# An encoder block of attention and recurrence: its woven stage put in order by estimates that also follow PSUM banks, with copies moved to ScalarE and two transfers changed

## The chip, the cores and the metric

The kernel runs on one core of one Trainium2 chip. Its metric is the device time of one execution in microseconds (us). The engines are named as in the profile: PE is TensorE (PEld its weight loads), DVE is VectorE, ACT is ScalarE, POOL is GpSimd, and SP is the queue that issues the transfers.

## What is computed

One layer on a sequence of 1024 positions with 1024 channels, in float32. A combined projection feeds two branches. Their sum, gated, is merged and added to the input, and a gated feed-forward part with a convolution of width 3 follows.

```
h = rms_norm(x, norm_mix_g)
mla_cols, rw_cols, gate_cols = split(h @ w_in)
o_a = mla_branch(mla_cols, ...)      # 8 heads: softmax(q k' + rope) v over all 1024 positions
o_b = rwkv7_branch(rw_cols, ...)     # 8 heads of 64: a forward and a backward scan,
...                                  #   state = state*w + (state a) b' + v k',  out = state r
y = sig(gA) * (o_a @ w_o[:512]) + sig(gB) * (o_b @ w_o[512:])
x = x + y @ w_merge
x = x + (silu(dwconv(h2 @ w_ffn_gate)) * (h2 @ w_ffn_up)) @ w_ffn_down     # h2 = rms_norm(x)
```

## The kernel before

The work has three stages. First come the projections and what prepares both branches. The second stage, which starts where `written` is entered (line 785) and ends at line 1628, weaves two things into one order of instructions: the **recurrence** and the **dense work**. The third is the merge and the feed-forward part; nothing in it is changed.

**Dense work** is the generator `dense`: the last gate projections (`gates`), then `attention` (line 1264), then `branch0` (line 1422), the first branch's product with the output weights `w_o`. Large products are split: a float32 operand x goes in as a rounded part `hi` and a remainder `lo`, and three matmuls hi·hi, hi·lo, lo·hi replace one. Attention takes 8 heads with 16 steps each (two halves of the queries by 8 blocks of keys). A step multiplies keys by queries into a PSUM bank `st` (three of them), ACT takes the exponential, and DVE or POOL forms the remainder `pl` of the rounded probabilities `ph`. Four steps later (`LAG`, line 48) `values` (line 1268) multiplies both by the values into the one bank `po`. On odd steps ACT takes the exponential twice, into `ph` and in place, and DVE subtracts; on even steps ACT writes the exponential `pe` into a buffer `wraw`, rounds it into `ph`, and POOL subtracts. At a head's last block the sum of values is copied out of `po` to `pv` by DVE and its logarithm to `rc` by ACT (lines 1283 and 1284).

While a head runs, `maxima` (line 1238) finds the row maxima for the next head: 16 products into banks `sc`, each reduced by DVE (`mx`), two in each of the steps 3 to 10; in step 11 a small DVE maximum and in step 12 a transpose on PE, after which ACT writes the negated maxima `mr`. They go by one transfer to a buffer `dm` in DRAM (line 1257) and by a second into row 96 of the next head's queries `qh` (line 1258). The next head's queries and keys are loaded in step 0 of a head (`load_h`, line 1219).

**The recurrence** runs over 8 units of 128 positions. For each, `prep_a` (line 834) makes decays and the inverse of a triangular matrix, the last part of it in four small steps on PE that the planner calls p, x, y and t; they write `TT`, `U` and `Y`, and their results are copied out of the banks alternately by DVE and ACT (lines 946, 957, 967). `prep_b` (line 971) makes further operands (`Er`, `Ek`, `BT`). `chain` (line 1035) is the serial part, 7 hops a unit, with results in banks of the same ring `sc` (four banks, line 800) under the name `ct`; one hop copies both halves of the new state out of `ct`, one half by DVE into `RR[0]` and the other by ACT into `RR[1]`. `gnorm` (line 1115) normalizes the unit's output `osb`: a product into `sc`, two activations there by ACT (`rsqrt_`), four multiplications and an addition by DVE, a product with the gates' weights, and from unit 4 on a sum and a split whose last part goes out of `osb` to `d_ob` in DRAM.

**The order** is fixed when the program is written: PE, DVE, ACT and POOL get their instructions in exactly the order in which these generators issue them. The planner at line 1580 picks the next piece by a model of time. `now` is PE's time; the wrapper `Clocked` (line 91) adds each DVE, ACT or POOL instruction's estimated duration to that engine's time, and `Fed` (line 111) notes when a matmul's operands are ready. A job of the preparation is due when its operands are estimated ready; a hop of the chain when its input is ready and enough dense work (`DENSE`) has gone by; otherwise the next dense piece is taken (`fill`). `dense_at` is the time at which the next `values` has its operands. If it lies later than `now[0] + 200`, dense work counts as blocked, and hops and heavy preparation steps go first. The model knows nothing of banks that are still occupied, and nothing of transfers. SP's order is not written by hand here; its instructions still wait in a line, each for its own data or buffer.

Of the kernel before, what the change touches and what calls it, by code (L numbers as in the profile page):

```python
# [10 lines left out]
F32 = mybir.dt.float32  # L11
# [55 lines left out]
DENSE_MIN = 1300  # L67
CT_BUFS = 2

# [17 lines left out]
def block_kernel(ctx: ExitStack, tc: tile.TileContext, a):  # L87
    nc = tc.nc
    now, ends, needs_pe, wrote = [0.0], [0.0], [0.0], {}

    class Clocked:


        def __init__(self, eng, fixed, each):
            self.eng, self.fixed, self.each, self.t = eng, fixed, each, 0.0

        def __getattr__(self, name):
            f = getattr(self.eng, name)

            def call(*args, **kw):  # L100
                o = kw["in_"] if name == "tensor_reduce" else kw["out"] if "out" in kw else args[0] if args else None
                if hasattr(o, "shape"):
                    out = kw["out"] if "out" in kw else args[0]
                    names = [x.tensor.name for x in (*args, *kw.values()) if x is not out and hasattr(x, "tensor")]
                    self.t = max(self.t, now[0], *(wrote.get(x, 0) for x in names)) + self.fixed + self.each * math.prod(o.shape[1:])
                    ends[0] = max(ends[0], self.t)
                    wrote[out.tensor.name] = self.t
                return f(*args, **kw)  # L108
            return call

    class Fed:
# [5 lines left out]
        def __getattr__(self, name):  # L117
            f = getattr(self.eng, name)

            def call(out, a, b, **kw):  # L120
                needs_pe[0] = max(needs_pe[0], wrote.get(a.tensor.name, 0), wrote.get(b.tensor.name, 0))
                wrote[out.tensor.name] = 0
                return f(out, a, b, **kw)  # L123
            return call

    E = Fed(nc.tensor)
    V, S, G = Clocked(nc.vector, 140, 1.04), Clocked(nc.scalar, 140, 0.92), Clocked(nc.gpsimd, 100, 2.35)
    mult, add, sub = ALU.mult, ALU.add, ALU.subtract
# [114 lines left out]
    def rsqrt_(out, ss, scale, bias):  # L243
        act(out, ss, AF.Ln, scale=scale, bias=bias)
        act(out, out, AF.Exp, scale=-0.5)
# [542 lines left out]
    now[0] = V.t = S.t = G.t = 0.0  # L788
    wrote.clear()
    wpool["g"] = ctx.enter_context(pool("gp", side="right"))  # L790
# [43 lines left out]
    def prep_a(n, q):  # L834
# [109 lines left out]
        for g in range(4):  # L944
            r, b = 32 * g, 32 * (g % 2)
            (S.copy if g % 2 else V.tensor_copy)(TT[r:r + 16, :, b + 16:b + 32], py[r:r + 16])
        yield 1600, 300
# [7 lines left out]
        for h in range(2):  # L955
            ib = slice(h * 64 + 32, h * 64 + 64)
            (S.copy if h else V.tensor_copy)(Y[ib], p3[ib])
        yield 1100, 300
# [6 lines left out]
        for h in range(2):  # L965
            ia = slice(h * 64, h * 64 + 32)
            (S.copy if h else V.tensor_copy)(TT[ia, :, 32:64], p3[ia])
        q.update(TT=TT)
# [66 lines left out]
    def chain(n, q, osb):  # L1035
# [30 lines left out]
        for i in range(2):  # L1066
# [14 lines left out]
            for s, d, c in EACH:  # L1081
                for hs in H:
                    E.matmul(ct[hs, s, :], TT[hs, 8 * i + s, :], rh[hs, s, :], start=(s == 0), stop=(s == 7))
            V.tensor_copy(RR[0][H[0], :, 1, :], ct[H[0]])
            S.copy(RR[1][H[1], :, 1, :], ct[H[1]])
# [29 lines left out]
    def gnorm(n, osb):  # L1115
        if n == NU // 2:
            xb.extend([[place(f"h{x}{4 + p}", f"ob{x}") for x in "hl"] for p in range(NPAIR - 1)])
        for d in range(2):
# [13 lines left out]
            if n >= NU // 2:  # L1132
                ob = wk.tile([128, 512], F32, tag="gsq", name="gob")
                nc.sync.dma_start(ob.rearrange("p (c t) -> p c t", t=128), d_obf[:, :, cs])
            rsqrt_(ps, ps, 1.0 / 64, gneps)
            rs = osb[:, d, :].rearrange("p (c t) -> p c t", t=128)
            for p in range(NPAIR):
                V.scalar_tensor_tensor(out=rs[:, p], in0=rs[:, p], scalar=vc("lng", p), in1=ps[:, 128 * p:128 * p + 128], op0=mult, op1=mult)
            V.tensor_tensor(out=b3, in0=rs if d == 0 else rs[:, :, ::-1], in1=b3, op=add)
            yield 540, 300  # L1140
            ps = scb()
# [96 lines left out]
    def maxima(h):  # L1238
        qh, kh = qk[h % 2]
        pt = scb  # L1240
        mx2 = eq.tile([128, 8, 2], F32, tag="mx2", name="mx2")
        for qt in range(8):
            for i2, hs in enumerate(halves()):
                ps = pt()
                E.matmul(ps, qh[0:96, qt * 128:(qt + 1) * 128], kh[0:96, hs], start=True, stop=True)
                V.tensor_reduce(out=mx2[:, qt, i2:i2 + 1], in_=ps, axis=AX_X, op=ALU.max)
                yield 213
        mx = eq.tile([128, 8], F32, tag="mx", name="mx")
        V.tensor_tensor(out=mx, in0=mx2[:, :, 0], in1=mx2[:, :, 1], op=ALU.max)
        yield 0  # L1250
        pm = pt()
        E.transpose(pm[0:8, 0:128], mx, ident)
        eq.tile([128, 8], F32, tag="pad", name="pad")
        mr = eq.tile([8, 128], R, tag="mr", name="mr")
        S.activation(mr, pm[0:8, 0:128], AF.Copy, scale=-1.0)
        dm = dr.tile([8, 128], F32, tag="dm", name="dm", bufs=2)
        nc.sync.dma_start(dm, mr.bitcast(F32))
        nc.sync.dma_start(qh[96:97, :].bitcast(F32), dm.rearrange("a b -> (a b)")[None, :])
        yield 213

    o0, o3 = [], []
    dense_at = [0.0]

    def attention():
# [3 lines left out]
        def values(h, q2, kt, ph, pl):  # L1268
# [10 lines left out]
            if kt == 7:  # L1279
                if i == 0 and q2 == 0:  # L1280
                    po["v"], po["r"] = (place(x, n, F32, [128, 2, 512]) for x, n in (("hl7", "pv"), ("hh7", "rc")))
                pv, rc = po["v"][:, q2], po["r"][:, q2]
                V.tensor_copy(pv[own], po[0][own])
                act(rc[own], po[0][oth], AF.Ln)
                po["t"] = max(V.t, S.t)
                if i == 1:
# [23 lines left out]
        def low():  # L1310
            eng, pl, x, ph = lows.pop(0)
            eng.tensor_tensor(out=pl, in0=x, in1=ph.bitcast(F32), op=sub)

        for h in range(8):
            qh, kh = qk[h % 2]
            nxt = maxima(h + 1) if h < 7 else iter(())
            for q2 in range(2):
                qs = HT[q2]
                for kt in range(8):
# [9 lines left out]
                    cost = 640  # L1329
                    for _ in range(2 if 3 <= step < 11 else 1 if step in (11, 12) else 0):  # L1330
                        cost += next(nxt, 0)
# [11 lines left out]
                    else:  # L1343
                        ph, pl = (wpool["g3"].tile([128, 512], R, tag=t, name=n) for t, n in (("gt", "ph"), ("gl", "pl")))
                    if npl[0] % 2:
                        act(ph, ps, AF.Exp)
# [16 lines left out]
                    if len(late) == LAG and late[0][2]:  # L1363
                        after()
                    yield cost
        low()
        queue.extend([lambda br=br, j=j: wrows(w_o(br, j), 0, NPAIR) for br, j in [*((0, j) for j in range(8)), (1, 0)]])
        for i in range(LAG):
# [9 lines left out]
    def wrows(src, k, n):  # L1378
        return wload(src[:, k * 128:min(k + 4, n) * 128], 128 * min(4, n - k), bufs=2)

    def w_o(br, j):
# [88 lines left out]
    LATER = ("er", "ak", "bt")  # L1470
    HEAVY = ("nm", "nz", "p", "x", "y", "t", "er", "ak", "bt")
    seen = {}
    due, hops, ready = 0.0, 0, 0.0
# [18 lines left out]
    class Job:  # L1492
# [5 lines left out]
        def due(self):  # L1498

            step, _, eng = self.steps[self.k]  # L1500
            t = max(self.at, eng.t - SLACK if eng else 0)
            if self.i:
# [77 lines left out]
    for u in range(NU):  # L1580
        osb = None if u else wk.tile([128, 2, 512], F32, tag="osb", name="osb")
        ch = chain(u, qs_[u], lambda: osb)
        for k in range(9):
            want = [(u, None, "t"), (u, 0, "bt")] if k == 0 else [(u, 1, "bt")] if k == 3 else []
            sparse = 0
            while True:
                t = max([ready] + [seen.get(x, math.inf) for x in want])
                thin = sparse_()
                blocked = dense_at[0] > now[0] + 200
                if t <= now[0] and (blocked or due <= 0 and not thin):  # L1590
# [616 lines left out]
```

## Time and profile before

| | us |
|---|---|
| median of 3 runs (lowest, highest) | 1910.35 (1905.93, 1911.68) |
| profiled execution, its own time | 1902.57 |
| its span, first to last instruction | 1900.8 |

The page gives each engine's busy time and, in 40 slices of 47.5 us, how busy it was; the line PEclk is the share of TensorE's full clock that was granted. The recurrence lies from about 366 to 1063 us of the span, attention from about 631 to 1024 us, and the product with `w_o` follows. Of the chain of work that ended last, only the part from 953 us on is a single thread; in the woven stage PE is nearly always the engine at work, and the question there is when PE stands still.

### The profile page before, as it was taken

The page shows a single profiled execution, that of the slowest core. Times are in us where ns is not written, and L with a number is a line of the kernel's source. Part 1 is how long each engine was busy: PE and PEld are TensorE (multiplying, and loading weights), DVE is VectorE, ACT ScalarE, POOL GpSimd, SP SyncE. Part 2 cuts the span into 40 slices and gives each one's busy share as a digit, 9 for nine tenths or more (in the row PEclk, how much of TensorE's full clock was granted, in tenths as well). Part 3 has the DMA queues.
Part 4 walks back from the last instruction along what each step waited for, and adds up shares of the span by engine and source line. Part 5 has one row for each costly group of instructions (what it writes and reads, how often), then busy time and mean ns, then how long its engine had stood idle before and what let it go on. Part 6 is the DMA issues. An engine that isn't in the chain of part 4 may idle for free. (4 is left out here: it accounts for less than half of the span.)

```text
span 1900.8 us, 36763 instructions
## 1 busy us (share of the span) xinstructions
PE 1821.6 (96%) x14928; PEld 1457.5 (77%) x14928; DVE 1214.8 (64%) x1867; ACT 865.6 (46%) x1387; POOL 634.1 (33%) x559
## 2 busy tenths in 40 slices
PE   8899999999999998988998999999999999999998
PEld 6666667888787877766776877878888888888886
DVE  5956666445566686767573363688675766757667
ACT  5776566223233466655666544543332323323231
POOL 2434555322222324352533322336223222222221
PEclk9999999999999899998999999999999999999999
DMA  4146444844455445453434682111111111111112
GB/s 171 45 145 221 159 161 161 239 134 106 131 142 139 125 107 146 103 141 84 98 93 146 206 300 81 63 49 56 50 51 51 54 63 51 50 51 51 59 47 105
DMA packets 260633, 210.65 MB, mean 111 GB/s; under 512 B 127145, under 2 KB 205033, under 8 KB 260465
## 3 DMA queue, kind: packets, MB, share of 16 engines
q1 hardware_dynamic: 260464, 208.31, 36.4%
q8 instruction: 117, 1.92, 0.4%
q14 instruction: 52, 0.42, 0.1%
HBM read 144.64 MB, written 59.41 MB: 107 GB/s over the span
## 5 line engine op out<-in xcount | busy, mean ns | idle before, releaser
L108 POOL TENSOR_TENSOR wlo<-wraw,whi 128x512 fp32r<-128x512 f32 x118 | 164.1, 1391 | 564.0 <-ACT whi L108 561.7
L123 PE MATMUL st<-hh,whi 128*128 128x512 f32 x408 | 170.6, 418 | 10.3 <-ACT hh L108 8.6
L123 PE MATMUL st<-hl,whi 128*128 128x512 f32 x408 | 162.5, 398 | 0.5 <-DVE hl L108 0.5
L108 DVE TENSOR_TENSOR x<-b,x 128x512 f32<-128x512 f32 x176 | 119.0, 687 | 53.4 <-PE b L123 53.4
L123 PE MATMUL st<-hh,wlo 128*128 128x512 f32 x408 | 139.5, 396 | 0.6 <-POOL wlo L108 0.6
L108 POOL TENSOR_TENSOR pl<-pe,ph 128x512 fp32r<-128x512 f32 x64 | 83.1, 1301 | 162.6 <-ACT ph L108 134.0
L108 ACT CAST whi<-wraw 128x512 fp32r<-128x512 f32 x118 | 72.9, 618 | 133.7 <-issue 39.0
L123 PEld LDWEIGHTS st<-hh,whi 128*128 128x128 f32 x408 | 77.9, 191 | 37.3 <-issue 10.4
L108 DVE TENSOR_REDUCE mx<-sc 128x1 f32<-128x512 f32 x128 | 81.9, 683 | 27.2 <-PE sc L123 27.0
L123 PEld LDWEIGHTS st<-hh,wlo 128*128 128x128 f32 x408 | 78.1, 192 | 18.5 <-POOL wlo L108 1.0
L123 PEld LDWEIGHTS st<-hl,whi 128*128 128x128 f32 x408 | 78.2, 192 | 16.9 <-issue 1.2
L108 POOL TENSOR_TENSOR wl<-wraw,wh 128x512 fp32r<-128x512 f32 x22 | 28.9, 1314 | 173.1 <-ACT wh L108 173.1
L108 DVE TENSOR_TENSOR u<-b,p 128x512 f32<-128x512 f32 x42 | 29.0, 691 | 70.6 <-PE b L123 70.6
L123 PE MATMUL b<-sl,wh 128*128 128x512 f32 x176 | 68.6, 390 | 0.8 <-DVE sl L108 0.8
L123 PE MATMUL b<-sh,whi 128*128 128x512 f32 x176 | 68.6, 390 | 0.7 <-DVE x L108 0.7
L123 PE MATMUL b<-sh,wh 128*128 128x512 f32 x176 | 68.6, 390 | 0.6 <-ACT sh L108 0.6
L123 PE MATMUL b<-sh,wl 128*128 128x512 f32 x176 | 68.5, 389 | 0.0
L123 PE MATMUL b<-sh,wlo 128*128 128x512 f32 x176 | 68.5, 389 | 0.0
L123 PE MATMUL b<-sl,whi 128*128 128x512 f32 x176 | 68.5, 389 | 0.0
L108 DVE TENSOR_TENSOR pl<-st,ph 128x512 fp32r<-128x512 f32 x64 | 43.7, 685 | 29.7 <-ACT st L108 29.4
L108 ACT CAST whi<-s 128x512 fp32r<-128x512 f32 x33 | 20.6, 623 | 87.2 <-PE b L123 87.2
L123 PE MATMUL po<-ph,vhh 128*128 128x512 f32 x128 | 57.2, 447 | 1.8 <-ACT rc L108 1.8
(488 smaller groups left out, 5298.1 us busy)
## 6 DMA issues: line engine op xcount, KB each, us to landing
wraw<-w_in SPq DMA_DIRECT2D x64, 256.0 KB
wraw<-w_fd SPq DMA_DIRECT2D x44, 256.0 KB
AA<-w_fu SPq DMA_DIRECT2D x41, 256.0 KB
A<-w_fg SPq DMA_DIRECT2D x41, 256.0 KB
d_gate<-gt SPq DMA_DIRECT2D x32, 256.0 KB
ld<-d_x SPq DMA_DIRECT2D x32, 256.0 KB
xt<-xT SPq DMA_DIRECT2D x8, 512.0 KB
d_s<-sg SPq DMA_DIRECT2D x8, 512.0 KB
```

What stands on the lines that cost most here:

```text
L108: return f(*args, **kw)
L123: return f(out, a, b, **kw)
```

## The change

1. **The model of time.** Each tile of the tags `sc`, `st`, `po`, `whi` and `wlo` belongs to a ring of so many buffers (`RING`); `slot` gives the time at which the tile that had the same buffer before was last used, and an instruction or matmul that writes a tile is now estimated to start no earlier. A job whose step needs a bank (`BANKS`) is not due before `vacant("sc")`. DVE and POOL instructions with two operands in SBUF are modelled as excluding each other (`port`).
2. **The planner's test for blocked dense work** becomes `dense_at[0] > now[0] - 800` in place of `+ 200`: operands must be estimated ready for 0.8 us.
3. **`gnorm`** gives way (`yield 540, 0`) between the two activations and DVE's multiplications, and the planner comes back to it when ACT is estimated done.
4. **Copies go to ACT alone**: those of p to t (`TT`, `Y`), the half of the state that DVE copied (`RR[0]`), and `pv`.
5. **Maxima**: `mr` is written to row 96 of `qh` by one transfer, without `dm`. The transpose is issued in the first step after 11 in which the last maximum is estimated ready, and in step 14 at the latest.
6. **Output weights**: in the last four steps of attention (the two even ones among them) the remainder is formed from PSUM by DVE, so that `wraw` is free, and the first block of `w_o` is loaded after step 5 of the last half head; its split (`wsplit`) takes the place in the queue at which it was loaded before.

The diff, cut to its core:

```diff
-CT_BUFS = 2
+RING = {"sc": 4, "st": 3, "po": 1, "whi": 2, "wlo": 2}
...
+    def slot(t):
+        if t.name not in prior:
+            tag = t.tag.split("_")[0]
+            q, n = order.setdefault(tag, []), RING.get(tag, 0)
+            prior[t.name] = q[-n] if 0 < n <= len(q) else None
+            q.append(t.name)
+        return used.get(prior[t.name], 0)
+    def vacant(tag):
+        q = order.get(tag, [])
+        return used.get(q[-RING[tag]], 0) if len(q) >= RING[tag] else 0
...
-                    self.t = max(self.t, now[0], *(wrote.get(x, 0) for x in names)) + self.fixed + self.each * math.prod(o.shape[1:])
+                    self.t = max(self.t, now[0], slot(out.tensor), *(wrote.get(x, 0) for x in names))
...
+                    if shared:
+                        self.t = max([self.t] + [e for b, e in self.port[1 - self.side] if b <= self.t])
+                        begin = self.t
+                    self.t += self.fixed + self.each * math.prod(o.shape[1:])
...
-                needs_pe[0] = max(needs_pe[0], wrote.get(a.tensor.name, 0), wrote.get(b.tensor.name, 0))
+                needs_pe[0] = max(needs_pe[0], slot(out.tensor), wrote.get(a.tensor.name, 0), wrote.get(b.tensor.name, 0))
...
-            (S.copy if g % 2 else V.tensor_copy)(TT[r:r + 16, :, b + 16:b + 32], py[r:r + 16])
+            S.copy(TT[r:r + 16, :, b + 16:b + 32], py[r:r + 16])
...
-            (S.copy if h else V.tensor_copy)(Y[ib], p3[ib])
+            S.copy(Y[ib], p3[ib])
...
-            (S.copy if h else V.tensor_copy)(TT[ia, :, 32:64], p3[ia])
+            S.copy(TT[ia, :, 32:64], p3[ia])
...
-            V.tensor_copy(RR[0][H[0], :, 1, :], ct[H[0]])
+            S.copy(RR[0][H[0], :, 1, :], ct[H[0]])
...
             rsqrt_(ps, ps, 1.0 / 64, gneps)
+            yield 540, 0
...
-            yield 540, 300
+            yield 0, 300
...
-        dm = dr.tile([8, 128], F32, tag="dm", name="dm", bufs=2)
-        nc.sync.dma_start(dm, mr.bitcast(F32))
-        nc.sync.dma_start(qh[96:97, :].bitcast(F32), dm.rearrange("a b -> (a b)")[None, :])
+        nc.sync.dma_start(qh[96:97, :].bitcast(F32), mr.bitcast(F32))
...
-                V.tensor_copy(pv[own], po[0][own])
+                S.copy(pv[own], po[0][own])
...
-                    for _ in range(2 if 3 <= step < 11 else 1 if step in (11, 12) else 0):
+                    for _ in range(2 if 3 <= step < 11 else 1 if step == 11 or step > 11 and mx_at[0] <= now[0] + cost or step == 14 else 0):
...
-                    if npl[0] % 2:
+                    if npl[0] % 2 or h == 7 and q2 and kt > 3:
...
+                    if h == 7 and q2 and kt == 5:
+                        raw = wpool["w"].tile([128, 512], F32, tag="wraw", name="wraw")
+                        wpool["load"] = nc.sync.dma_start(raw, w_o(0, 0))
...
-        queue.extend([lambda br=br, j=j: wrows(w_o(br, j), 0, NPAIR) for br, j in [*((0, j) for j in range(8)), (1, 0)]])
+        queue.append(lambda: wsplit(raw))
+        queue.extend([lambda br=br, j=j: wrows(w_o(br, j), 0, NPAIR) for br, j in [*((0, j) for j in range(1, 8)), (1, 0)]])
...
-            t = max(self.at, eng.t - SLACK if eng else 0)
+            t = max(self.at, eng.t - SLACK if eng else 0, vacant("sc") if step in BANKS else 0)
...
-                blocked = dense_at[0] > now[0] + 200
+                blocked = dense_at[0] > now[0] - 800
```

More of the change, by code (lines that the diff above doesn't have):

```diff
@@ L89, in block_kernel, with __init__ @@
     now, ends, needs_pe, wrote = [0.0], [0.0], [0.0], {}
+    used, order, prior = {}, {}, {}
+    def slot(t):
[8 more added lines that the diff above has]
+        return used.get(q[-RING[tag]], 0) if len(q) >= RING[tag] else 0
     class Clocked:
-        def __init__(self, eng, fixed, each):
-            self.eng, self.fixed, self.each, self.t = eng, fixed, each, 0.0
+        def __init__(self, eng, fixed, each, port=None, side=0):
+            self.eng, self.fixed, self.each, self.t, self.port, self.side = eng, fixed, each, 0.0, port, side
         def __getattr__(self, name):
@@ L104, in call @@
                     names = [x.tensor.name for x in (*args, *kw.values()) if x is not out and hasattr(x, "tensor")]
-                    self.t = max(self.t, now[0], *(wrote.get(x, 0) for x in names)) + self.fixed + self.each * math.prod(o.shape[1:])
+                    self.t = max(self.t, now[0], slot(out.tensor), *(wrote.get(x, 0) for x in names))
+                    data = [str(kw[x].tensor.space) for x in ("in0", "in1") if hasattr(kw.get(x), "tensor")]
+                    shared = self.port is not None and len(data) == 2 and "PSUM" not in data
+                    if shared:
+                        self.t = max([self.t] + [e for b, e in self.port[1 - self.side] if b <= self.t])
+                        begin = self.t
+                    self.t += self.fixed + self.each * math.prod(o.shape[1:])
+                    if shared:
+                        self.port[self.side].append((begin, self.t))
+                        del self.port[self.side][:-8]
                     ends[0] = max(ends[0], self.t)
                     wrote[out.tensor.name] = self.t
+                    for x in (out.tensor.name, *names):
+                        used[x] = max(used.get(x, 0), self.t)
                 return f(*args, **kw)
@@ L120, in call @@
             def call(out, a, b, **kw):
-                needs_pe[0] = max(needs_pe[0], wrote.get(a.tensor.name, 0), wrote.get(b.tensor.name, 0))
+                needs_pe[0] = max(needs_pe[0], slot(out.tensor), wrote.get(a.tensor.name, 0), wrote.get(b.tensor.name, 0))
+                for x in (a, b, out):
+                    used[x.tensor.name] = max(used.get(x.tensor.name, 0), now[0], needs_pe[0])
                 wrote[out.tensor.name] = 0
@@ L126, in block_kernel @@
     E = Fed(nc.tensor)
-    V, S, G = Clocked(nc.vector, 140, 1.04), Clocked(nc.scalar, 140, 0.92), Clocked(nc.gpsimd, 100, 2.35)
+    port = ([], [])
+    V, S, G = Clocked(nc.vector, 140, 1.04, port, 0), Clocked(nc.scalar, 140, 0.92), Clocked(nc.gpsimd, 100, 2.35, port, 1)
     mult, add, sub = ALU.mult, ALU.add, ALU.subtract
@@ L788, in block_kernel @@
     now[0] = V.t = S.t = G.t = 0.0
-    wrote.clear()
+    for x in (wrote, used, order, prior):
+        x.clear()
+    for x in port:
+        x.clear()
     wpool["g"] = ctx.enter_context(pool("gp", side="right"))
@@ L1249, in maxima @@
         V.tensor_tensor(out=mx, in0=mx2[:, :, 0], in1=mx2[:, :, 1], op=ALU.max)
+        mx_at[0] = wrote[mx.tensor.name]
         yield 0
@@ L1255, in maxima @@
         S.activation(mr, pm[0:8, 0:128], AF.Copy, scale=-1.0)
-        dm = dr.tile([8, 128], F32, tag="dm", name="dm", bufs=2)
-        nc.sync.dma_start(dm, mr.bitcast(F32))
-        nc.sync.dma_start(qh[96:97, :].bitcast(F32), dm.rearrange("a b -> (a b)")[None, :])
+        nc.sync.dma_start(qh[96:97, :].bitcast(F32), mr.bitcast(F32))
         yield 213
     o0, o3 = [], []
-    dense_at = [0.0]
+    dense_at, mx_at = [0.0], [0.0]
     def attention():
@@ L1282, in values @@
                 pv, rc = po["v"][:, q2], po["r"][:, q2]
-                V.tensor_copy(pv[own], po[0][own])
+                S.copy(pv[own], po[0][own])
                 act(rc[own], po[0][oth], AF.Ln)
-                po["t"] = max(V.t, S.t)
+                po["t"] = S.t
                 if i == 1:
@@ L1379, in wrows, with wsplit @@
         return wload(src[:, k * 128:min(k + 4, n) * 128], 128 * min(4, n - k), bufs=2)
+    def wsplit(raw):
+        hi, lo = (wpool["w"].tile([128, 512], R, tag=t, name=t, bufs=2) for t in ("whi", "wlo"))
+        split(raw, hi, lo)
+        return hi, lo
     def w_o(br, j):
@@ L1471, in block_kernel @@
     HEAVY = ("nm", "nz", "p", "x", "y", "t", "er", "ak", "bt")
+    BANKS = ("nm", "nz", "p", "x", "y", "t", "er", "ak", "bt")
     seen = {}
```

## The prediction

> **What bounds the kernel now.** I read the page's busy shares first, then a table of stretches, then PE's own list of waits, then the waits of ACT and DVE that lie behind those.
>
> ```profile
> PE 1821.6 (96%) x14928; PEld 1457.5 (77%) x14928; DVE 1214.8 (64%) x1867; ACT 865.6 (46%) x1387; POOL 634.1 (33%) x559
> ```
>
> ```profile
> 366.00:1063.10 697.10, 662.38 (x9992) 533.19 (x9987) 426.26 (x842) 343.07 (x618) 222.17 (x243) 0.97 0.48 124
> 640.00:1020.00 380.00, 353.71 (x5055) 281.11 (x5053) 265.45 (x501) 237.66 (x438) 147.50 (x155) 0.97 0.44 108
> ```
>
> The page says that PE is busy for 96% of the span, so the kernel is bound by PE's work, which the change leaves as it is. What can be won lies in the woven stage. The first row of the second block is that stage, the second its part with attention (start and end, length, then PE, PEld, DVE, ACT and POOL, the granted clock, the share and rate of the transfers). PE stands still for 697.1 - 662.4 = 34.7 us of the stage; 380 - 353.7 = 26.3 us of it lie in attention. A granted clock of 0.97 over 697 us costs 0.03 x 697 = about 21 us more (17 to 24 with the rounding). So about 56 us is the most that any order of this stage could win, 3% of the kernel.
>
> PE's own waits, from just before the stage (320 us) to 1100 us, say who ended each stop (total us, how often, longest):
>
> ```profile
> PE sc L123 <- issue: 6.9, 3, 3.1
> PE sc L123 <- DMA qh<-d_qrh: 6.2, 3, 4.0
> PE st L123 <- ACT whi L108: 4.7, 1, 4.7
> PE sc L123 <- DVE mx L108: 4.1, 3, 2.2
> PE sc L123 <- ACT osb L108: 4.0, 1, 4.0
> PE po L123 <- DVE pl L108: 1.9, 2, 1.4
> PE po L123 <- ACT rc L108: 1.8, 2, 1.6
> PE sc L123 <- ACT gsq L108: 1.2, 1, 1.2
> PE sc L123 <- DMA Un<-dU: 1.1, 1, 1.1
> ...
> PE po L123 <- POOL pl L108: 0.6, 1, 0.6
> PE sc L123 <- ACT RR L108: 0.5, 1, 0.5
> ```
>
> I sort them in three. One stop of 4.7 us is the first output weight. DVE `mx`, DVE and POOL `pl`, ACT `rc`, `gsq` and `RR`, together 4.1 + 1.9 + 0.6 + 1.8 + 1.2 + 0.5 = 10.1 us, are matmuls issued before a result was there or before a bank was empty: this is what the planner's model of time decides. The rest, 6.9 + 6.2 + 4.0 + 1.1 = 18.2 us, are instructions that waited for nothing visible and transfers, of which the model knows nothing, before or after.
>
> A stop costs more than its length:
>
> ```profile
> 856.50:866.70 10.20, 9.62 (x55) 7.45 (x57) 8.01 (x19) 5.58 (x12) 1.27 (x1) 0.50 0.11 26
> 887.20:890.60 3.40, 3.25 (x8) 2.50 (x9) 2.20 (x4) 0.00 (x0) 1.11 (x1) 0.50 1.08 221
> 1023.70:1027.10 3.40, 2.91 (x8) 1.87 (x10) 0.00 (x0) 1.96 (x4) 2.55 (x2) 0.50 1.03 417
> ```
>
> These three stretches stand right behind the three stops of 4 us and more (`osb`, `qh<-d_qrh`, `whi`). In each the clock is granted at 0.50, for 10.2, 3.4 and 3.4 us, so half of that, 5.1, 1.7 and 1.7 us, is lost on top. [...]
>
> **The change part by part.** *Output weights (part 6).* Time of start, duration, engine, instruction:
>
> ```profile
> 1018.70 0.38 SPq L220 DMA_DIRECT2D wraw<-w_o  x1
> ...
> 1023.52 0.62 ACT L108 CAST whi<-wraw 128x512 fp32r<-128x512 f32 x1 [4.84 <-DMA wraw<-w_o]
> ...
> 1024.19 2.08 PE L123 MATMUL st<-o,whi 128*128 128x512 f32 x4 [4.74 <-ACT whi L108]
> ```
>
> The load goes out at 1018.70, is rounded 4.8 us later, and PE stands for 4.74 us. Issued after step 5 of the last half head, some three steps before attention's end, the load can land before PE needs it. The stop and its clock are worth 4.7 + 1.7 = 6.4 us. Behind it the second weight block and the second operand (`o` of 1 MB) come next, on the same transfers; so I take 5, with 1 and 6.4 as ends. That DVE forms two of the remainders which POOL made costs it 2 x 0.68 us (first row below, shortest, median and longest in ns), beside other work.
>
> ```profile
> L108 DVE TENSOR_TENSOR pl<-st,ph x64: 673/682/693, 636.2 to 1016.0; 128x512 fp32r<-128x512 f32 x64
> ```
>
> ```profile
> L108 DVE COPY pv<-po x16: 673/688/695, 669.1 to 1019.5; 64x512 f32<-64x512 f32 x16
> ```
>
> ```profile
> L108 DVE COPY Y<-sc x8: 683/683/684, 413.9 to 1016.7; 32x512 f32<-32x512 f32 x8
> L108 ACT COPY Y<-sc x8: 578/579/582, 414.6 to 1017.4; 32x512 f32<-32x512 f32 x8
> ```
>
> *Copies on ACT (part 4).* The waits of ACT and DVE on each other, and the copies themselves:
>
> ```profile
> ACT TT L108 <- DVE TT L108: 53.2, 23, 9.6
> ACT RR L108 <- DVE RR L108: 42.0, 14, 6.4
> ...
> ACT rc L108 <- DVE pv L108: 20.8, 14, 4.2
> ...
> ACT Y L108 <- DVE Y L108: 13.7, 8, 5.4
> ```
>
> ```profile
> L108 DVE COPY TT<-sc x24: 411/422/680, 409.5 to 1029.4; 16x256 f32<-16x256 f32 x16, 32x512 f32<-32x512 f32 x8
> L108 ACT COPY TT<-sc x24: 363/366/583, 409.9 to 1030.1; 16x256 f32<-16x256 f32 x16, 32x512 f32<-32x512 f32 x8
> ```
>
> ```profile
> L108 DVE COPY RR<-ct 64x512 f32<-64x512 f32 x16 | 10.8, 678 | 8.0 <-PE ct L123 8.0
> ...
> L108 ACT COPY RR<-ct 64x512 f32<-64x512 f32 x16 | 9.3, 582 | 42.1 <-DVE RR L108 42.0
> ```
>
> ACT's copy waits for DVE's of the same bank nearly every time: 53.2 + 42.0 + 20.8 + 13.7 = 129.7 us in 59 waits, in which the exponentials queued behind it wait too. Put on one engine the pair needs no such wait. ACT takes on 16 x 0.37 + 8 x 0.58 (`TT`) + 8 x 0.58 (`Y`) + 16 x 0.58 (`RR`) + 16 x 0.58 (`pv`, of the same size as `RR`) = 34 us; DVE gives up 16 x 0.42 + 8 x 0.68 + 8 x 0.68 + 16 x 0.68 + 16 x 0.68 = 39 us. In attention ACT is busy 237.7 of 380 us; if two thirds of the 34 us fall there, it comes to 260, or 69%, which still leaves room. Two copies one behind the other take 1.16 us where DVE and then ACT took 0.68 + 0.58 = 1.26 and a semaphore: no loss for the chain. By itself this is worth nothing on PE beyond the waits counted above; it makes the estimates easier to keep.
>
> [...] Where two such copies ran beside each other, one engine would be slower; here the wait rows say that they ran one after the other. This is a rival below.
>
> *`gnorm` gives way (part 3).*
>
> ```profile
> DVE osb L108 <- ACT sc L108: 54.9, 15, 9.1
> ```
>
> DVE stood 15 times, 3.7 us on average, before the multiplications until ACT had done its two activations, with `mx`, `pl` and copies of banks queued behind them. After the change the planner puts other DVE work there. It is what stands behind several of the `mx` and `pl` stops.
>
> *Banks in the model, and the 0.8 us (parts 1 and 2).* They aim at the 10.1 us of my second group, by filling with recurrence work until the operand is there. The estimates will not always hold; I take two thirds, 6.5 us. From both sides: none of it, or all 10.1 us. The clock of the stage besides the three stretches quoted has lost 21 - 8.5 = 12 us in shorter stops and phases of small matmuls; I take 2 of that, and 0 and 6 as ends.
>
> *Maxima (part 5).*
>
> ```profile
> SPq L1258 <- DMA dm<-mr: 8.0, 7, 1.4
> ```
>
> SP, whose queue holds the loads of keys, queries and values, stands 8.0 us in 7 waits for the first of the two transfers to land. That goes. PE never waits for row 96 by the list above, so the transfer itself is worth nothing; SP's release may shorten the 6.2 us of `qh<-d_qrh`, but `load_h` is issued two or three steps later. I take 1 us, with 0 and 3 as ends. A transpose that is issued as late as step 14 leaves two steps until the next head reads row 96. Two steps last 6 us on average (380 us for 128 of them), more than the 4.8 us of the weights' load, so mostly nothing is late; I take a loss of 0.5, with 0 and 7 (1 us at each of seven head changes) as ends.
>
> *The third group, 18.2 us, and its clock.* New order deals these anew. The 4.0 us for `osb` came when ACT had to wait for the store of the unit before; with its 5.1 us of clock it is 9.1 us, in one place. A norm with one more step per direction ends neither clearly earlier nor later. I take 2 us as a gain here, with a loss of 6 and a gain of 9 as ends.
>
> **Sum.** 5 + 6.5 + 2 + 1 - 0.5 + 2 = 16 us. Against the profiled execution's own 1902.6 us this is 1886.6. That execution lay 7.8 us under the median of the runs, 1910.35, by which I forecast: 1894. What a measurement of this kernel can tell from no change is about 0.3%, or 5.7 us.
>
> **The rivals.**
>
> *The stops move instead of going.* The planner still sees no transfer, and the third group is larger than the second. If the two groups trade places, only the output weights and SP's waits are left: 1910.35 - 6 = 1904, or with half of them given back 1907. For it speaks that 18.2 of 34.7 us idle are outside the model; against it, that DVE's 54.9 us and ACT's 129.7 us in line go for a reason that is not a matter of luck.
>
> *Slower: bare steps at the change of heads.*
>
> ```profile
> 882.96 0.58 SPq L1223 DMA_DIRECT2D qh<-d_qrh  x1
> ...
> 887.35 1.19 PE L123 MATMUL sc<-kh,qh 96*128 96x512 f32 x2 [3.99 <-DMA qh<-d_qrh]
> ```
>
> The next head's queries are asked for in step 0 and read in step 3; here the load took 4.4 us from its issue, and PE stood 3.99 us. With the new test blocked dense work lets hops and preparation run earlier, so the recurrence gets ahead and has less left to lay between the steps 0 and 3 of later heads. Each such change then costs 4.0 + 1.7 = 5.7 us. There are six changes of heads with such a load; if all six stood bare, that is 34.2 less the 6.2 + 1.7 of now, 26 us more, and 1894 + 26 = 1920. At the fifth bare change the gain of 16 is gone (5 x 5.7 - 7.9 = 20.6); only all six give a loss over 5.7 us. Against it:
>
> ```profile
> L108 ACT COPY osb<-ct x16: 581/587/589, 436.7 to 1062.4; 128x512 f32<-128x512 f32 x16
> ```
>
> the recurrence's last output leaves its bank at 1062.4 us, 38 us behind the first product with `w_o` at 1024.19, so there is work left over to the end, and the model, now with waits for banks in it, holds jobs back as well as forward.
>
> [...] If the pairs of copies could have run side by side, one engine alone makes 16 `RR` pairs longer by 1.16 - 0.68 = 0.48 us, 16 pairs of long `TT` and `Y` copies the same (8 + 8), and 16 short pairs by 0.73 - 0.42 = 0.31 us: 15.4 + 5.0 = 20 us. If all of that came onto PE, 1894 + 20 = 1914. The 59 waits speak against it.
>
> *The change doesn't do what it says:* the early load could stay behind others in SP's queue (before, it went out at 1018.70 behind two loads and a store), and then 5 of the 16 us are missing: 1899.
>
> **How the numbers follow.** The forecast and its neighbour without the early weights hold 0.70, both over 5.7 us faster; the moved stops 0.17, of which 0.03 lie just beyond the bound on the fast side; bare head changes 0.09; ACT as the bound 0.04, of which 0.01 stays within the bound. The best case takes every gain's end, but of the clock only the 2: 6.4 + 10.1 + 9 + 3 + 2 = 30.5, or 1880. On the other side I reach to 1912, which takes in the moved stops and leaves out bare head changes and the worst of ACT. So 1880 to 1912; faster 0.73, same 0.15, slower 0.12.
>
> **What would show it.** Right: PE's list without the stop before the first `st<-o,whi` and with `mx`, `pl` and `rc` under 4 us together; no wait of ACT for DVE on `TT`, `RR`, `rc`, `Y`; DVE's wait for ACT before `osb` under 15 us; PE idle in the woven stage near 23 us with a clock of 0.98. Wrong: stops for `qh<-d_qrh` or for row 96 that grew, a long stop at `osb`, or PE's idle time unchanged with other names in the list. Were the three named groups gone and the time still the same, the clock or the small matmuls would hold what I ascribe to waiting.

## The result and the profile after

The kernel after takes 1917.51 us (median of 8 runs, 1914.12 to 1920.98), beside 1909.66 us for the kernel before (8 runs, 1903.23 to 1912.77). The ratio is 1.0054, with a 95% interval of 1.0038 to 1.0070: the change made the kernel about 8 us slower, where a gain of 16 us was forecast. The profiled execution of after took 1914.12 us with a span of 1912.3 us, 11.5 us more than the span of before.

The first part of the page of after gives each engine's busy time:

```profile
PE 1827.0 (96%) x14928; PEld 1463.4 (77%) x14928; DVE 1177.4 (62%) x1805; ACT 896.8 (47%) x1451; POOL 629.2 (33%) x557
```

PE issues the same 14,928 matmuls. DVE gave up 37 us and ACT took on 31 us, as worked out beforehand (39 and 34). So the difference has to be sought in when PE stands still and at what clock it runs. Two tables of stretches, first of before, then of after, each with the whole woven stage (first `sc` to first `b`) and with attention (first `st<-qh,kh` to first `st<-o,whi`):

```profile
365.68:1089.13 723.45, 688.73 (x10113) 554.43 (x10113) 437.62 (x862) 360.02 (x642) 231.57 (x254) 0.97 0.48 127
631.20:1024.19 392.99, 362.51 (x5240) 288.15 (x5239) 272.02 (x511) 243.31 (x449) 150.08 (x157) 0.97 0.45 111
```

```profile
369.56:1102.63 733.07, 691.65 (x10108) 558.11 (x10107) 401.31 (x802) 391.85 (x706) 227.83 (x252) 0.97 0.48 126
629.60:1035.22 405.62, 376.34 (x5658) 303.01 (x5656) 253.65 (x480) 270.06 (x503) 147.65 (x156) 0.95 0.44 108
```

The stage grew by 9.6 us. PE stands still for 733.07 - 691.65 = 41.4 us of it, before for 723.45 - 688.73 = 34.7 us. The rest is clock: half-clock stretches cover 51.2 us of the stage in after, 41.0 us in before (10 and 7 stretches), and half of each is counted as lost, 25.6 against 20.5 us (a little too much, since PE also stands still in some of them). Idle time and lost clock together grew by 6.7 + 5.1 = 11.8 us, which more than covers the stage's 9.6. The 3.9 us by which the stage starts later are not the change's: its start lies between 365.7 and 370.6 us over all 18 traces, whatever the version; what follows the stage took 2.0 us less, and so the span grew by 11.5.

PE's own waits in after, from 320 to 1110 us (total us, how often, longest):

```profile
PE sc L151 <- issue: 10.3, 6, 2.6
PE sc L151 <- DVE mx L134: 7.7, 6, 2.6
PE sc L151 <- DMA qh<-d_qrh: 4.2, 3, 1.8
PE sc L151 <- ACT osb L134: 2.9, 1, 2.9
PE st L151 <- DMA qh<-mr: 2.8, 2, 2.0
PE st L151 <- issue: 2.6, 2, 1.9
PE b L151 <- ACT obh L134: 2.6, 1, 2.6
PE st L151 <- ACT pe L134: 2.5, 1, 2.5
PE po L151 <- POOL obl L134: 2.2, 1, 2.2
PE ct L151 <- ACT RR L134: 1.1, 2, 0.7
PE po L151 <- ACT rc L134: 1.1, 1, 1.1
```

The stop before the first output weight is gone, but `mx`, which the model of banks was to shorten, went from 4.1 to 7.7 us, "issue" from 6.9 to 12.9, and there are new names: `qh<-mr`, `obh`, `pe`, `obl`. Before, 8 stops of the stage lasted over 1.5 us; now 12 do. All of PE's waits for another engine's result together, without the weights' and ACT's `osb`, went from 12.9 to 18.7 us by the full lists.

The waits of DVE and ACT on each other did go, as foreseen. From their lists in after:

```profile
DVE osb L134 <- ACT sc L134: 17.6, 4, 9.4
```

```profile
ACT TT L134 <- PE sc L151: 34.3, 11, 8.0
ACT RR L134 <- PE sc L151: 23.7, 13, 3.4
```

DVE's 54.9 us before the multiplications of `gnorm` became 17.6. ACT's copies to `TT`, `RR` and `Y` now wait for PE alone; no wait for DVE on `TT`, `RR`, `rc` or `Y` is left. So these parts of the change did what they say, and PE still stands longer.

### The profile page after: what moved, and what is told of

Its sections match the earlier page's. It is cut to its first block, busy times and chain, and to the rows that moved or that the text cites. A ratio compares the mean times of both kernels' runs of the same rounds, so it can differ in the third digit from the quotient of the medians.

```text
span 1912.3 us, 36801 instructions
## 1 busy us (share of the span) xinstructions
PE 1827.0 (96%) x14928; PEld 1463.4 (77%) x14928; DVE 1177.4 (62%) x1805; ACT 896.8 (47%) x1451; POOL 629.2 (33%) x557
## 3 DMA queue, kind: packets, MB, share of 16 engines
q8 instruction: 117, 1.92, 0.4%
## 4 chain that ended last, share of the span: by engine, by line
PE 71%; DVE 5%; DMA 2%; issue 2%; ACT 2%; POOL 1%; SPq 1%; ACTq 0%; POOLq 0%; DVEq 0%
PE b L151 37%; PE st L151 13%; PE sc L151 10%; PE po L151 7%; PE ct L151 4%; DVE x L134 1%; DMA qh<-d_qrh 1%; DVE u L134 1%; DVE wlo L134 0%; DMA y<-d_gate 0%; DVE mx L134 0%; DVE b L134 0%; DVE wl L134 0%; DMA d_obf<-gbo 0%; DMA wraw<-w_in 0%
## 5 line engine op out<-in xcount | busy, mean ns | idle before, releaser
L151 PE MATMUL st<-qh,kh 128*128 128x512 f32 x128 | 57.1, 446 | 5.5 <-DMA qh<-mr 2.8
L134 ACT CAST whi<-s 128x512 fp32r<-128x512 f32 x33 | 20.5, 623 | 87.2 <-PE b L151 87.2
```

## The experiments

Two theories stood at first: the loss comes from the new order of PE, or it comes from the edits themselves (a longer chain on ACT, a transpose too late). Then, with the order found to be at fault, two more: the model of banks makes bad orders (A1 in the texts on record), or any newly planned order is a draw from a wide scatter (A2).

All times are medians beside the kernel before on the same chip (1906.2 to 1909.1 us over four groups of runs). "Idle" is PE's idle time in the woven stage, "lost clock" half of its half-clock stretches, both of the profiled execution.

### Edits and order apart

The change edits instructions and also lets the planner choose another order. To part the two, the planner's choices were recorded as a list of pieces and the kernel follows the list instead of choosing:

```diff
-                blocked = dense_at[0] > now[0] + 200
...
-                x = prepare(not blocked and (thin or sparse and t < math.inf), not blocked and 0 < alone[0] < BATCH and due > -math.inf)
...
+            while (p := next(plan)) != "c":
+                norm.run() if p == "n" else fill() if p == "f" else jobs[ord(p) - 65].run()
```

PE's list of instructions in after differs from that of before: some 1500 instructions stand in another place. With the list of before, every one stands where it stood. **e1** is before with its own order as a list.

> The kernel before, with its sequence of pieces written out as a list in place of the planner's choices; every engine's order is unchanged. Both theories: 1909 us, within 0.3% of before. Its profile tells which stops of PE come back from run to run at the same place (those that the order makes) and which do not: I expect the stops for osb, qh and the first output weight again within 0.5 us, and stops that wait for nothing visible at other places or of other lengths.

It took 1909.39 us, ratio 0.9999 (0.9981 to 1.0017): within that interval the list itself costs nothing. **e2** holds PE's order of before and has the edits that need no new order: the copies on ACT (part 4), the maxima by one transfer (of part 5, without the later transpose), the early output weights (part 6).

```diff
-            V.tensor_copy(RR[0][H[0], :, 1, :], ct[H[0]])
+            S.copy(RR[0][H[0], :, 1, :], ct[H[0]])
...
-        nc.sync.dma_start(dm, mr.bitcast(F32))
-        nc.sync.dma_start(qh[96:97, :].bitcast(F32), dm.rearrange("a b -> (a b)")[None, :])
+        nc.sync.dma_start(qh[96:97, :].bitcast(F32), mr.bitcast(F32))
...
+                        wpool["load"] = nc.sync.dma_start(raw, w_o(0, 0))
```

> The pieces in exactly the order of before on PE, with the edits alone: copies on ACT, maxima by one transfer (transpose in step 12 as before), early output weights. Theory A (the new order is what costs, the edits by themselves win): about 1903 us, 6 less than before, the stop of 4.7 us before the first product with the output weights gone. Theory B (copies on ACT cost, by ACT's longer line): about 1917 us, with ACT's exponentials late in PE's list.

It took 1892.47 us, ratio 0.9904 (0.9873 to 0.9936), less than either theory had expected. **e3** is the reverse: PE's order of after as a list, with the copies, the two transfers and the late output weights of before.

> The pieces in exactly the order of after on PE, with the old copies, two transfers for the maxima and the late output weights. Theory A: slower than after by what the edits win, about 1923 us. Theory B: faster than after, about 1909 us.

It took 1928.16 us, ratio 1.0093 (1.0068 to 1.0118). The four corners, in us (ratios above; after with its own order is the 1.0054 of the result):

| | order of before | order of after |
|---|---|---|
| edits of before | 1909 | 1928 (e3) |
| edits of after | 1892 (e2) | 1918 |

The edits gain in either order, 16 us in the old and 11 us in the new one. The new order costs 19 us without them and 25 us with them. (After was timed beside another chip's kernel before. By the ratios, which compare on one chip, the edits gain 18 and 7 us, and the order costs 18 and 29.) PE's waits in e2 over the same 320 to 1110 us, and its attention as a stretch:

```profile
PE sc L123 <- DMA qh<-d_qrh: 5.9, 3, 4.0
PE sc L123 <- issue: 4.8, 2, 2.5
PE sc L123 <- ACT osb L108: 4.6, 1, 4.6
PE sc L123 <- DMA Un<-dU: 2.0, 1, 2.0
PE po L123 <- DVE pl L108: 1.4, 1, 1.4
PE sc L123 <- ACT gsq L108: 1.2, 1, 1.2
PE po L123 <- POOL pl L108: 1.1, 1, 1.1
...
PE st L123 <- ACT whi L108: 0.6, 1, 0.6
...
PE sc L123 <- DVE mx L108: 0.4, 1, 0.4
PE ct L123 <- ACT RR L108: 0.3, 1, 0.3
```

```profile
634.08:1013.26 379.18, 361.16 (x5241) 289.23 (x5239) 251.70 (x472) 263.69 (x489) 147.68 (x155) 0.97 0.46 113
```

All stops over 1 us that e2 still has, but for one of 1.06 us (`pl`), stood at the same places before; `mx` fell from 4.1 to 0.4 us, `rc` from 1.8 to nothing, the output weights from 4.7 to 0.6. Idle time in attention fell from 392.99 - 362.51 = 30.5 to 379.18 - 361.16 = 18.0 us. PE's order is untouched, so this is only operands, banks and weights that were there earlier.

The waits speak against the rival with ACT as the bound, in which the pairs of copies could have run side by side: with the copies dealt to both engines, as in e3, ACT's list shows

```profile
ACT TT L134 <- DVE TT L134: 54.2, 23, 8.4
...
ACT RR L134 <- DVE RR L134: 29.8, 13, 4.2
```

and in the order of before the edits that put them on one engine are part of the 16 us won (e2; the copies were not run apart from the other two edits).

**e4** is after with the old test, planned anew.

```diff
-                blocked = dense_at[0] > now[0] - 800
+                blocked = dense_at[0] > now[0] + 200
```

> After, with the planner's test for blocked dense work as before (+ 200 in place of - 800); the planner chooses anew. If the 0.8 us are what costs: about 1909 us, and the clock lost in attention back from 20 to near 10 us. If the order costs for another reason (banks in the model, or any new deal): 1915 to 1920 us, as after.

1923.45 us, ratio 1.0071 (1.0049 to 1.0094). Without the 0.8 us the planner dealt no better order; how much one such deal can tell, the later runs show.

### Is it the model of banks?

**e5** has the edits of e2, but the planner of before chooses again. The edits alone, above all the copies' new engine, change its choices.

> The edits (copies on ACT, maxima by one transfer, early weights) with the planner of before, which chooses its order anew since the copies changed engines. Theory A1 (the new model of banks makes the bad order): about 1893 us, as with the old order held fixed. Theory A2 (the old order was a lucky one, and any new deal by either planner lands some 10 to 25 us above it): 1903 to 1918 us.

1907.23 us, ratio 0.9999 (0.9977 to 1.0022). The same instructions as e2, the same planner as before, and the 16 us are gone: merely dealing the order again cost them. **e6** adds part 3, `gnorm`'s extra step.

```diff
+            yield 540, 0
...
-            yield 540, 300
+            yield 0, 300
```

> The same and the norm giving way before DVE's multiplications, still with the old model and the old test. A1: 1888 to 1893 us, since DVE's wait for ACT before osb goes. A2: anywhere from 1895 to 1918 us.

1923.15 us, ratio 1.0080 (1.0056 to 1.0103), with this row at the head of PE's waits:

```profile
PE sc L123 <- DMA qh<-d_qrh: 21.8, 4, 11.8
```

This is the rival of bare steps at the change of heads; it is real, but it struck here and not in after, where that wait is 4.2 us. **e7** is after without its model of banks: nothing is held to wait for a bank or a port.

```diff
-        return used.get(prior[t.name], 0)
+        return 0
...
-        return used.get(q[-RING[tag]], 0) if len(q) >= RING[tag] else 0
+        return 0
...
-    V, S, G = Clocked(nc.vector, 140, 1.04, port, 0), Clocked(nc.scalar, 140, 0.92), Clocked(nc.gpsimd, 100, 2.35, port, 1)
+    V, S, G = Clocked(nc.vector, 140, 1.04), Clocked(nc.scalar, 140, 0.92), Clocked(nc.gpsimd, 100, 2.35)
```

> After, without the model's part for rings, vacant banks and the shared port; the test at 0.8 us, the norm and all edits stay. A1: about 1893 us, 25 less than after. A2: no nearer to 1893 than after is, 1905 to 1920.

1890.86 us, ratio 0.9910 (0.9886 to 0.9935). **e8** keeps the model and takes the other planning parts back (+200, the old `gnorm`, the old transpose steps).

> The edits with the new model of banks alone: the test at + 200, the norm and the step of the transpose as before. A1: about 1917 us, as after. A2: 1903 to 1918 us, not clearly apart from the other deals.

1941.83 us, ratio 1.0183 (1.0154 to 1.0212). Two pairs now said that the model costs 27 us (e7 to after) and 35 us (e5 to e8). That looked like the cause; the next runs were made to test it.

### Or is any new order a draw?

In what follows a constant of the planner is changed by 30 ns: the estimated time of a hop (`HOP`) or the margin on a result (`MARGIN`), both 300 ns. The work on the chip stays the same; the planner merely chooses differently here and there. **e9** is e7 with a hop of 330 ns.

```diff
-HOP = 300
+HOP = 330
```

> After without the model of banks, with one planner constant moved by 30 ns (the time added after a hop, 300 to 330), which deals the pieces anew. Theory A1 (the model of banks is what costs): 1891 us again, within 6. Theory A2 (scatter of deals): anywhere from 1885 to 1920 us.

1931.93 us, ratio 1.0117 (1.0088 to 1.0146): 30 ns in an estimate made the best kernel of the study 41 us slower. **e10** is after with a margin of 330 ns; **e11** is after without `vacant`; **e12** is after with only the port left of the model (`slot` and `vacant` give 0).

> After with another planner constant moved by 30 ns (the margin behind an estimated end, 300 to 330): a new deal with the model of banks. A1: 1917 us again, within 6. A2: anywhere from 1890 to 1935 us.

> After, whose jobs no longer wait for a vacant bank; the model still lets instructions start no earlier than their bank is free, and still has the shared port. If holding jobs back is the harm (a step that would empty its bank in time is put off behind dense work): near 1891 us. If the later estimated starts are: 1917 us as after.

> After with only the shared port of DVE and POOL left in the model. If the rings of banks are the harm: near 1891 us; if the port's estimates are: near 1917 us. A2 again expects no pattern, 1890 to 1930 us.

They took 1927.99 (1.0099, 1.0069 to 1.0130), 1936.13 (1.0146, 1.0119 to 1.0174) and 1927.6 us (1.0099, 1.0068 to 1.0129). The parts of the model do not add up to anything: without one part it is slower, without all it is faster. What e7 has and e9 lacks, by PE's waits, first e7, then e9:

```profile
PE sc L151 <- issue: 11.8, 7, 3.1
PE sc L151 <- DVE mx L134: 6.8, 7, 1.9
PE b L151 <- ACT obh L134: 2.6, 1, 2.6
PE sc L151 <- DMA qh<-d_qrh: 2.3, 1, 2.3
```

```profile
PE sc L151 <- issue: 12.3, 8, 3.2
PE sc L151 <- DVE mx L134: 9.6, 4, 5.1
PE sc L151 <- DMA qh<-d_qrh: 6.7, 3, 2.8
PE st L151 <- ACT whi L134: 4.3, 2, 3.5
PE sc L151 <- ACT gsq L134: 2.5, 2, 1.3
```

No one wait makes the difference. Most are longer or new, two are gone (`obh`, 2.6 us, and one for `o`, 2.3 us), the whole list has 14 rows in place of 10, and idle time goes from 26.9 to 52.4 us, lost clock from 18.8 to 39.3.

Two more orders of each family followed: **e13** and **e14** are e7 with a hop of 270 ns and a margin of 330 ns, **e15** and **e16** are after with a hop of 330 and of 270 ns.

> The kernel after without its model of banks, and with the estimated time of a hop at 270 ns in place of 300 (the constant is in the planner alone; the work is the same). So far with the same edits: with the model of banks whole 1917.5 and 1928.0; without it 1890.9 and 1931.9. Theory A1, the model of banks makes orders that are worse by themselves: both kernels without it in this call lie under both kernels with it, near 1891 to 1905. Theory A2, any new order is drawn from a wide scatter and the model of banks does not decide it: between 1890 and 1940, the four kernels of this call mixed, means of the two families within 10 us of each other.

> The kernel after without its model of banks, and with the planner's margin at 330 ns in place of 300. A1: 1891 to 1905, under both kernels with the model. A2: anywhere from 1890 to 1940.

> The kernel after, model of banks whole, with the estimated time of a hop at 330 ns in place of 300. A1: 1915 to 1940, over both kernels without the model. A2: anywhere from 1890 to 1940. If this change of 30 ns moved the kernel by under 3 us, the model of banks would at least make the order insensitive, against A2.

> The kernel after, model of banks whole, with the estimated time of a hop at 270 ns in place of 300. A1: 1915 to 1940, over both kernels without the model. A2: anywhere from 1890 to 1940.

| ratio to before (95%) | model of banks | none |
|---|---|---|
| as in after / e7 | 1.0054 (1.0038, 1.0070) | 0.9910 (0.9886, 0.9935) |
| margin 330 (e10 / e14) | 1.0099 (1.0069, 1.0130) | 1.0070 (1.0047, 1.0093) |
| hop 330 (e15 / e9) | 1.0087 (1.0060, 1.0114) | 1.0117 (1.0088, 1.0146) |
| hop 270 (e16 / e13) | 1.0031 (1.0016, 1.0047) | 0.9996 (0.9979, 1.0012) |
| mean | 1.0068 | 1.0023 |

In the last group of runs, from the shortest time to the longest, the model was absent, present, absent, present (1908.74, 1916.51, 1922.11, 1927.10 us). The means lie 0.0045 apart, 9 us; four draws that scatter by 0.009 (none) and 0.003 (with) fix that difference only to about 0.005. Counting e4 and e8 with the model and e5 and e6 without it, six orders against six lie 0.0059 apart, fixed to about 0.004. So the model of banks is not shown to matter by itself, and the theory as it was put on record, every order without it better than every order with it, falls; a cost of some us is not excluded. A2 comes off better, but its own ranges were too narrow: e6, e8 and e9 came out above them, e7 below. What holds: a new order acts like a draw from a wide scatter. The 14 orders that a planner chose anew with the edits in them (after, e4 to e16) lie from 0.9910 to 1.0183, with a mean of 1.0067 and a standard deviation of 0.0068, 13 us. The order of before, with the same edits, gives 0.9904, 31 us under that mean. Only e7 comes near it.

### What an order's stops cost

Over the 18 profiled executions (before, after, e1 to e16), idle time and lost clock of the woven stage vary from 42.1 us (e2) to 103.0 us (e8), and the span follows them with a correlation of 0.98. Some of them, in us:

| | e2 | e7 | before | e5 | after | e6 | e9 | e11 | e8 |
|---|---|---|---|---|---|---|---|---|---|
| PE idle | 23.3 | 26.9 | 34.7 | 33.3 | 41.4 | 48.6 | 52.4 | 57.6 | 55.3 |
| lost clock | 18.8 | 18.8 | 20.5 | 30.7 | 25.6 | 35.8 | 39.3 | 39.3 | 47.8 |
| stops over 1.5 us | 6 | 9 | 8 | 9 | 12 | 12 | 13 | 17 | 19 |
| span | 1891.4 | 1890.8 | 1900.8 | 1904.7 | 1912.3 | 1919.7 | 1930.4 | 1937.7 | 1940.3 |

With each us of idle time goes 0.71 us of lost clock (sum over the 18). In after the steps of the clock look like this; three stretches of its table:

```profile
640.51:650.75 10.24, 9.46 (x53) 7.73 (x55) 4.92 (x11) 3.55 (x8) 1.26 (x1) 0.50 0.11 26
739.50:742.91 3.41, 3.41 (x12) 2.20 (x13) 0.69 (x1) 2.63 (x5) 0.00 (x1) 0.50 0.92 261
934.06:937.47 3.41, 2.75 (x7) 2.17 (x7) 0.00 (x0) 1.66 (x3) 1.64 (x4) 0.50 0.09 24
```

They begin near the ends of stops of 2.63 us (`mx`), 1.99 us (`qh<-mr`) and 2.17 us (`obl`), and the clock is at 0.50 for 10.24, 3.41 and 3.41 us. All ten half-clock stretches of the stage in after begin within 1.2 us of the end of a stop of 1.4 to 2.9 us. Not every such stop has one: none follows the 1.92 us before 747.86 us ("issue") and the 2.60 us before 1102.63 us (`obh`). So the length of a stop alone doesn't tell whether the clock is halved behind it: the 1.44 us before 817.13 us ("issue") go with a half-clock stretch of 3.41 us at 818.01.

## Why the prediction was wrong

**Right: what the edits remove.** With the order held, e2 won 16 us. The stop before the output weights is gone in after too. In time order the request, and the first product that needs the weights, which now shows no wait:

```profile
1020.73 0.38 SPq L1400 DMA_DIRECT2D wraw<-w_o  x1
```

```profile
1035.22 1.07 PE L151 MATMUL st<-o,whi 128*128 128x512 f32 x4
```

**Mis-ascribed: the second group.** Of its 10.1 us two thirds were to go "by filling with recurrence work until the operand is there", by parts 1 and 2. In e2 the group (`mx`, `pl`, `rc`, `gsq`, `RR`) is 0.4 + 1.4 + 1.1 + 1.2 + 0.3 = 4.4 us, so 5.7 us of it went, without parts 1 and 2. So the edits brought what was put down to the planner. Most likely, but not shown, it was the copies on one engine, since `mx`, `rc` and the wait of ACT for DVE behind them went; the three edits of e2 were not run one by one. The prediction counted the copies as "worth nothing on PE beyond the waits counted above", and made those waits hang on a better order. In after, with parts 1 and 2, `mx`, `pl` and `rc` are at 7.7 + 0 + 1.1 = 8.8 us, where "under 4" was to show the step right. With `RR` (1.1) and waits of the same kind under new names (`obh`, `pe`, `obl`, `rh`: 2.6 + 2.5 + 2.2 + 0.7) the group is at 17.9 us. The 6.5 us that parts 1 and 2 were to win did not come; the group grew.

**The step that failed: a new order as a small, two-sided term.** "New order deals these anew. ... I take 2 us as a gain here, with a loss of 6 and a gain of 9 as ends." Measured, the new order lost 25 us (e2 to after). The term was wrong in what it covered and in its size. All of the stage is dealt anew, not the third group alone; the standard deviation of a deal is 13 us, and the order of before, with the same edits, lay 31 us under their mean. That e2 lands at 1892, beside the forecast of 1894, is no support for the sum: its gain came with the order held and without parts 1 to 3. The third group itself came out at 10.3 + 2.6 + 4.2 + 2.9 + 2.8 = 22.8 us ("issue", `qh<-d_qrh`, `osb`, `qh<-mr`), 4.6 more than the 18.2 of before. The 2 us of clock to be gained became a loss of 5.1.

**The new transpose step** was given a loss of 0.5 us. Two of the seven head changes now stand bare for row 96:

```profile
736.33 0.73 SPq L1290 DMA_DIRECT2D qh<-mr  x1
...
738.32 0.47 PE L151 MATMUL st<-qh,kh 128*128 128x512 f32 x1 [1.99 <-DMA qh<-mr]
```

PE stands still from 736.33 us on, when the transfer is only just issued, and its row is there 2.0 us later. The two stops and the half-clock stretch at 739.50 make 2.8 + 1.7 = 4.5 us, inside the ends of 0 and 7. "The transfer itself is worth nothing" holds in the order of before only: in the order of after with the two old transfers (e3) the same wait was

```profile
PE st L151 <- DMA qh<-dm: 7.9, 2, 5.1
```

**`gnorm`.** DVE's wait before `osb` fell to 17.6 us, near the 15 set as a mark, but that it "stands behind several of the `mx` and `pl` stops" is not borne out. In after `mx` has the largest total of the named waits; and in e2, which leaves `gnorm` as it was, DVE waits as before,

```profile
DVE osb L108 <- ACT sc L108: 56.8, 15, 9.7
```

while PE's stops for `mx` fell from 4.1 to 0.4 us all the same.

**The rivals.** Bare head changes were priced for `qh<-d_qrh` at six places; after shows 4.2 us, less than before's 6.2. Moved stops came nearest in kind, but as a trade that leaves a gain. None of them had the order as a whole become worse; with the argument that 56 us is "the most that any order of this stage could win" the text looked at what an order could win and not at what it could lose: e8 stands at 103 us.

**What stays open.** Which of the moved instructions cost the 25 us; a part of the order was not exchanged alone. Why finer estimates don't choose better orders is only argued: over seven heads the planner of before reckons about 268 us where the trace has 345 (291 and 365 in after), so its time is off by a fifth or more with and without banks, and it knows of none of the transfers. Whether the order of before was a lucky draw or had another advantage can't be told from a single order; its planner was not run with a constant changed and the old edits.

The stops called "issue", 4.8 to 18 us in the 18 traces and with 12.9 us the largest group in after, end with nothing that the list of waits names. One of 2.42 us lies in the middle of small matmuls of one kind:

```profile
487.82 0.79 PE L151 MATMUL sc<-TT,P 32*16 32x16 f32 x71
491.03 0.58 PE L151 MATMUL sc<-TT,P 32*16 32x16 f32 x47 [2.42 <-issue]
```

The list of transfers gives a lead. Between 488.1 and 488.2 us, 2.9 us before this stop ends, a transfer starts on the queue that the page names "instruction" (packets, MB, share of 16 engines):

```profile
q8 instruction: 1, 0.02, 86.9%
```

In each of the 96 "issue" stops of over 1 us (320 to 1130 us, all 18 traces) a 16 KB transfer of this queue starts 2.2 to 3.4 us before the stop ends; of the 195 other stops of that length only 24 have one 2.1 to 3.5 us before their end. No run moved these transfers, so the coincidence is shown; that PE waits for them is not.

## What to carry to other kernels

When a change edits instructions and also lets a planner order them anew, measure the edits with the old order written out as a list, before the new order is looked at: here 16 us of gain were hidden under 25 us of loss, and the old order with the edits, 1892.47 us, is the version to keep, rather than e7 (1890.86), which a change of one constant undoes. Before a planner's new rule is believed or blamed, change an unrelated constant of it by a tenth a few times; a rule whose effect is smaller than that scatter, 13 us here, isn't shown by one pair of kernels, nor by two. And give "the order is dealt anew" a term of its own in the sum, with the scatter as its width and the mean of fresh orders, not the present order, as its centre.

## What the runs showed of the hardware

In after, PE's clock was granted at 0.50 near stops of 1.44 to 2.88 us: with one of 1.99 us went 3.41 us at half clock and with one of 2.63 us 10.24 us, so the stop of 1.99 us cost an estimated 3.7 us (1.99 and half of 3.41); stops of 1.92 and 2.60 us in the same trace had none. All 96 stops of PE of over 1 us that are called "issue" go with a 16 KB transfer of the queue named "instruction" that starts 2.2 to 3.4 us before their end. The small transfer of `mr` to a row of `qh` kept PE waiting until 2.0 us after its issue (736.33 to 738.32 us); in the same order the way by DRAM kept PE waiting for up to 5.1 us (e3), and SP waited for the first of its two transfers, 8.0 us in 7 waits in before. And the places of PE's longer stops came back from one run to another: e1, with before's order as a list, has all 13 stops of over 1 us of before at the same instructions and one more (`o`, 1.7): the output weights 5.2 us in place of 4.7, `osb` 3.9 in place of 4.0, `mx` 2.2 in both, only with other lengths where transfers are awaited (`Un` 3.2 in place of 1.1).
